# A mean over rows on one core: the first load issued in four parts of rows, and a branch hint for SyncE

## The chip, the cores and the metric

The kernel runs on one core of a Trainium2 chip. The metric is the device time of one execution in microseconds (us); the median of the runs is quoted. The kernel before takes between 1246.0 and 1246.5 us, with one run of 1247.15, so differences of a few tenths can be read, with care.

Some words: an engine *issues* a load; 16 DMA engines then carry it out in *packets*, in most loads here 65,536 B each, all that one partition holds of a block. The *tail* is what is left after the last bytes have landed. A *branch hint* is here an instruction near the start of an engine's program that names the branch at its end.

## The reference

```python
x = np.random.randn(64, 256, 8192).astype(np.float32)   # 536.9 MB
return np.mean(x, axis=2)                               # 16384 means of 8192 numbers
```

## The kernel before

The 16384 rows are taken in 64 blocks of 256 rows: 128 partitions, two rows of 32 KB side by side in each, so 64 KB to a partition and 8.39 MB to a block. Three buffers rotate. All loads are issued by SyncE, which does no sums here; all sums but a few at the end are VectorE's.

```python
x_v = x_f[0 : LB * P * R].rearrange("(p n r) s -> n p r s", p=P, r=R)
...
def load(dst, src, sem):
    ld = untracked(nc.sync.dma_start(out=dst, in_=src))
    ...
    ld.then_inc(sem, 16)

for n in range(LB):
    xt = slots[n % SLOTS]
    ld = load(xt[:], x_v[n], load_sem[n % LOAD_SEMS])
    if n == 0:
        first = ld
    if n < LB - 1:
        loaded(n, dve_sum(res[:, n * R : (n + 1) * R], xt[:]))
    ...   # the last of these blocks is shared with ScalarE
...       # the 64th block comes in pieces that get smaller: 4096, 2048, ... 256 columns
scaled_sum(fin[0][:, 0:1], head[:])
st = store_last(0)
with tc.issue_after(st.ins):
    st = nc.sync.wait_ge(tail_sem[-2], 16)
with tc.issue_after(st.ins):
    st = nc.sync.addr_align(FETCH_BLOCK, offset=0, max_nops=0)
untracked(scaled_sum(fin[1][:, 0:1], fin_in[:, 0 : lastw + k]))._wait_ge(sem, 16)
with tc.issue_after(st.ins):
    last_store = store_last(1)
```

After the build the first load is moved by hand ahead of the barrier that starts the program, so that it is SyncE's first instruction of weight. VectorE gets a branch hint for the branch at its end. `addr_align` in front of the last store is meant to align the place of the store's instruction in SyncE's program.

## Time and profile before

| | before |
|---|---|
| median of 6 runs, us | 1246.15 (1246.05 to 1246.41) |
| span of the profiled run, us | 1244.4 |
| bytes read | 536.87 MB |
| beat of a block in the steady part, us | 19.35 |
| first reduction starts, us | 22.07 |
| first data packet starts, us | 1.02 |

The timeline of VectorE at the start shows the beat. Columns: start, length, engine, line, operation, tiles, shapes, count, and in brackets the idle time before it and what ended it.

```profile
22.07 17.22 DVE L80 TENSOR_REDUCE res<-xt 128x2 f32<-128x16384 f32 x1 [21.07 <-DMA xt<-in_x_dram]
41.40 17.22 DVE L80 TENSOR_REDUCE res<-xt 128x2 f32<-128x16384 f32 x1 [2.11 <-DMA xt<-in_x_dram]
```

VectorE works for 17.22 us and waits for 2.1, every time for a load. The start of its first reduction is therefore a handy clock: whatever the first block loses is seen there, and everything behind it is a fixed beat. The view of SyncE's load line (minimum, median and maximum of an issue in ns) gives what an issue costs:

```profile
L70 SPq DMA_DIRECT2D xt<-in_x_dram x69: 327/328/435, 0.0 to 1202.6; - x69
```

### The profile page before, as it was taken

To read this page: it belongs to the slowest core of one execution; us is meant where nothing else is said; L and a number is where in the kernel's file an instruction comes from. 1 tells how busy PE (TensorE), PEld (TensorE's weight loads), DVE (VectorE), ACT (ScalarE), POOL (GpSimd) and SP (SyncE) were. 2 spreads that over 40 slices of the span, in tenths; PEclk is the share of its full clock that TensorE was granted. 3 is DMA by queue.
4 is the path that set the end of the run, shared out by engine and by line. 5 is a ranking of instruction groups with operands and counts; after the bars stand their busy time and mean duration, and the time that the engine had idled before them with its cause. 6 is when DMAs were issued, how large, how long until landed. Compare 5 with 4: busy or idle time off the path is not lost.

```text
span 1244.4 us, 203 instructions
## 1 busy us (share of the span) xinstructions
DVE 1087.0 (87%) x78; ACT 16.5 (1%) x13; POOL 0.2 (0%) x4
## 2 busy tenths in 40 slices
DVE  2898988989889889898898988989889898898898
ACT  0000000000000000000000000000000000000004
POOL 0000000000000000000000000000000000000000
DMA  9999999999999999999999999999999999999998
GB/s 432 423 426 438 438 438 438 436 430 415 438 438 438 438 438 432 417 432 438 438 438 438 432 417 432 438 438 438 438 436 419 426 438 438 438 438 436 426 419 373
DMA packets 10241, 536.95 MB, mean 431 GB/s; under 512 B 1280, under 2 KB 1536, under 8 KB 1792
## 3 DMA queue, kind: packets, MB, share of 16 engines
q1 hardware_dynamic: 10240, 536.94, 99.8%
q14 instruction: 1, 0.01, 0.0%
HBM read 536.87 MB, written 0.07 MB: 431 GB/s over the span
## 4 chain that ended last, share of the span: by engine, by line
DMA 70%; DVE 29%; SPq 0%; issue 0%; DVEq 0%
DMA xt<-in_x_dram 70%; DVE res L80 29%; DVE fin_in L80 0%; SPq L70 0%; DVE fin_in L86 0%; DVE fin_t L97 0%; DVEq L86 0%
## 5 line engine op out<-in xcount | busy, mean ns | idle before, releaser
L80 DVE TENSOR_REDUCE res<-xt 128x2 f32<-128x16384 f32 (+1 forms) x63 | 1076.3, 17085 | 153.1 <-DMA xt<-in_x_dram 153.1
L83 ACT ACT_TABLE_LOAD x1 | 1.3, 1283 | 1181.0 <-DVE res L80 1181.0
L83 ACT ACTIVATE xt<-xt 128x8192 f32<-128x8192 f32 (+5 forms) x6 | 14.7, 2444 | 43.9 <-DMA xt<-in_x_dram 43.7
L80 DVE TENSOR_REDUCE fin_in<-xt 128x1 f32<-128x256 f32 (+3 forms) x5 | 5.0, 1005 | 0.3 <-DMA xt<-in_x_dram 0.2
L80 DVE TENSOR_REDUCE head<-xt 128x1 f32<-128x4096 f32 x1 | 4.4, 4420 | 0.7 <-DMA xt<-in_x_dram 0.7
L83 ACT ACTIVATION_READ_ACCUMULATOR xt<-xt 128x1 f32 x6 | 1.1, 186 | 0.0
L60 DVE MEMSET fin<- 128x32 f32 x2 | 0.1, 85 | 0.9 <-PEq L238 0.9
L86 DVE TENSOR_SCALAR_CACHE_REDUCE fin_in<-fin_in 128x265 f32<-128x265 f32 x1 | 0.4, 430 | 0.2 <-DVE fin_in L80 0.2
L97 DVE STREAM_TRANSPOSE fin_t<-fin 128x32 f32<-128x32 f32 x2 | 0.4, 212 | 0.1
L138 DVE TENSOR_SCALAR bulk<-res 128x126 f32<-128x126 f32 x1 | 0.2, 228 | 0.1
L86 DVE TENSOR_SCALAR_CACHE_REDUCE head<-head 128x2 f32<-128x2 f32 x1 | 0.2, 154 | 0.1
L238 POOL MEMSET const-bfloat16-1.0<- 128x1 bf16 x1 | 0.1, 102 | 0.0
L238 POOL MEMSET const-uint8-127<- 128x1 uint8 x1 | 0.1, 102 | 0.0
L238 POOL MEMSET const-float32-0.0<- 128x1 f32 x1 | 0.1, 99 | 0.2 <-issue 0.2
L238 POOL MEMSET const-float32-1.0<- 128x1 f32 x1 | 0.1, 99 | 0.0
L86 DVE DVE_READ_ACCUMULATOR fin_in<-fin_in 128x1 f32 x1 | 0.1, 83 | 0.0
L86 DVE DVE_READ_ACCUMULATOR head<-head 128x1 f32 x1 | 0.1, 82 | 0.0
## 6 DMA issues: line engine op xcount, KB each, us to landing
xt<-in_x_dram SPq DMA_DIRECT2D x1, 4096.0 KB, 31.2
xt<-in_x_dram SPq DMA_DIRECT2D x1, 2048.0 KB, 35.7
xt<-in_x_dram SPq DMA_DIRECT2D x1, 1024.0 KB, 37.7
xt<-in_x_dram SPq DMA_DIRECT2D x63, 40.8
xt<-in_x_dram SPq DMA_DIRECT2D x1, 512.0 KB, 38.5
xt<-in_x_dram SPq DMA_DIRECT2D x1, 256.0 KB, 38.7
xt<-in_x_dram SPq DMA_DIRECT2D x1, 128.0 KB, 38.6
fin_in<-in_x_dram SPq DMA_DIRECT2D x1, 128.0 KB, 38.5
```

The source lines that it names most:

```text
L60: nc.vector.memset(fin[r][:], 0.0)
L80: return untracked(nc.vector.tensor_reduce(out=dst, in_=src, axis=X, op=ADD))
L83: return untracked(nc.scalar.activation(out=src, in_=src, func=COPY, accum_out=dst))
L86: return nc.vector.tensor_scalar(out=src, in0=src, scalar1=inv, scalar2=None, op0=mybir.AluOpType.mult, op1=ADD, accum_out=dst,)
L97: nc.vector.transpose(out=fin_t[r][:], in_=fin[r][:])
L138: nc.vector.tensor_scalar_mul(out=bulk[:], in0=res[:], scalar1=inv)
L238: nc = _bacc.Bacc("TRN2", target_bir_lowering=False, num_devices=1)
```

## The change

The intent: have the first data sooner by making the first load small, in parts of evenly spaced rows; and replace the wait and the alignment in front of the last store by a hinted branch for SyncE.

```diff
-FETCH_BLOCK = 128
+FIRST_PARTS = ((0, 8), (4, 8), (2, 4), (1, 2))
...
     def loaded(n, ins):
-        ins._wait_ge(load_sem[n % LOAD_SEMS], 16 * (n // LOAD_SEMS + 1))
+        more = len(FIRST_PARTS) - 1 if n % LOAD_SEMS == 0 else 0
+        ins._wait_ge(load_sem[n % LOAD_SEMS], 16 * (n // LOAD_SEMS + 1 + more))
...
-        ld = load(xt[:], x_v[n], load_sem[n % LOAD_SEMS])
-        if n == 0:
-            first = ld
+        for a, step in FIRST_PARTS if n == 0 else ((0, 1),):
+            ld = load(xt[a:P:step], x_v[n, a:P:step], load_sem[n % LOAD_SEMS])
+            if n == 0 and a == 0:
+                first = ld
...
-    with tc.issue_after(st.ins):
-        st = nc.sync.wait_ge(tail_sem[-2], 16)
-    with tc.issue_after(st.ins):
-        st = nc.sync.addr_align(FETCH_BLOCK, offset=0, max_nops=0)
...
# not the code, in short: before, VectorE's closing branch is made a hinted compare-and-branch;
# after, VectorE's and SyncE's, and the first load goes ahead of SyncE's first instruction
# (before: ahead of its drain in front of the start barrier)
```

So the first load becomes rows 0, 8, 16 ... (16 rows), 4, 12, 20 ... (16), 2, 6, 10 ... (32) and 1, 3, 5 ... (64).

More of the change, by code (lines that the diff above doesn't have):

```diff
@@ L157 @@
     head_bb, body_bb = nc.main_func.blocks[:2]
+    blocks = nc.main_func.blocks
+    end_bb, parent = blocks[2], nc.bb_map[body_bb.name]
+    hinted = {e.engine: e for e in (nc.vector, nc.sync)}
+    with nc.body("skipped", parent=parent, valid_engines=[*hinted]):
+        for eng in hinted.values():
+            eng.nop(nofuse=True)
+            eng.br(end_bb.name)
+    with nc.body("scratch", parent=parent, valid_engines=[*hinted]):
+        overs = [
+            eng.br_eq(eng.zero_reg, 0, end_bb.name, "skipped").ins
+            for eng in hinted.values()
+        ]
+    made = {b.name: b for b in blocks}
+    blocks.remove(made["scratch"])
+    blocks.remove(made["skipped"])
+    blocks.insert(2, made["skipped"])
+    for over in overs:
+        made["scratch"].instructions.remove(over)
+        plain = next(
+            i
+            for i in body_bb.instructions
+            if i.engine == over.engine and isinstance(i, mybir.InstUnconditionalBranch)
+        )
+        assert plain.target == end_bb.name
+        body_bb.instructions.insert(body_bb.instructions.index(plain), over)
+        body_bb.instructions.remove(plain)
+        hint = mybir.InstBranchHint(
+            name=nc.get_next_instruction_name(),
+            engine=over.engine,
+            associate_branch=over.name,
+        )
+        at = next(
+            i
+            for i, ins in enumerate(head_bb.instructions)
+            if ins.engine == over.engine and isinstance(ins, mybir.InstDrain)
+        )
+        head_bb.instructions.insert(at, hint)
     assert first.ins in body_bb.instructions
@@ L162 @@
         for i, ins in enumerate(head_bb.instructions)
-        if ins.engine == first.ins.engine and isinstance(ins, mybir.InstDrain)
+        if ins.engine == first.ins.engine
     )
     head_bb.instructions.insert(at, first.ins)
-    DVE = mybir.EngineType.DVE
-    blocks = nc.main_func.blocks
-    end_bb, parent = blocks[2], nc.bb_map[body_bb.name]
-    with nc.body("skipped", parent=parent, valid_engines=[DVE]):
-        nc.vector.nop(nofuse=True)
-        nc.vector.br(end_bb.name)
-    with nc.body("scratch", parent=parent, valid_engines=[DVE]):
-        over = nc.vector.br_eq(nc.vector.zero_reg, 0, end_bb.name, "skipped").ins
-    made = {b.name: b for b in blocks}
-    made["scratch"].instructions.remove(over)
-    blocks.remove(made["scratch"])
-    blocks.remove(made["skipped"])
-    blocks.insert(2, made["skipped"])
-    plain = next(
-        i
-        for i in body_bb.instructions
-        if i.engine == DVE and isinstance(i, mybir.InstUnconditionalBranch)
-    )
-    assert plain.target == end_bb.name
-    body_bb.instructions.insert(body_bb.instructions.index(plain), over)
-    body_bb.instructions.remove(plain)
-    hint = mybir.InstBranchHint(
-        name=nc.get_next_instruction_name(), engine=DVE, associate_branch=over.name
-    )
-    at = next(
-        i
-        for i, ins in enumerate(head_bb.instructions)
-        if ins.engine == DVE and isinstance(ins, mybir.InstDrain)
-    )
-    head_bb.instructions.insert(at, hint)
     exit_ins = list(end_bb.instructions)
```

## The prediction

The sum came to −0.33 us, so 1245.8 us in a range of 1245.1 to 1251.0. Its three terms all stand; the first, −0.40 us, is an estimate from the start times of the packets. Four rivals follow. The first is a lower rate of the small parts (small form: an engine's first two packets double, 20%; large form: all eight, 4%); its doubled packet was an assumption. The second is a first packet that stays as slow as before (25%), the third a wider gain. The fourth: a stall at SyncE's branch (3%). At the end, the signs of the first two rivals come right after those that would show the point right, in the same order.

> **What bounds the kernel now.** I read the page's busy shares and slices first, then its DMA queues, the chain of waits near the end, the stage table in steps of 0.2 us for the first microseconds, and the timeline of the tail.
>
> ```profile
> DVE 1087.0 (87%) x78; ACT 16.5 (1%) x13; POOL 0.2 (0%) x4
> ...
> DMA  9999999999999999999999999999999999999998
> ...
> q1 hardware_dynamic: 10240, 536.94, 99.8%
> ```
>
> The 16 DMA engines are busy for 99.8% of the span; VectorE has 13% to spare. The chain of the page mixes DMA and VectorE, because a load's issue waits for the reduction that frees its buffer. But that load then queues behind two others, so the reductions cost nothing. The timeline shows it: each reduction of a block takes 17.22 us and then VectorE waits 2.13 us for the next block, a beat of 19.35 us for 8.39 MB, or 433.5 GB/s.
>
> ```profile
> 22.05:41.40 19.35, 17.22 (x1) 0.00 (x0) 0.00 (x0) 1.00 1.00 434
> ...
> 600.00:619.35 19.35, 17.22 (x2) 0.00 (x0) 0.00 (x0) 1.00 1.00 434
> ```
>
> 64 blocks at 19.35 us are 1238.4 us of the 1244.4 us span. Only 6.0 us are left: the start before the engines run, and the tail. The change touches those alone. The start (columns: window, its length, VectorE, ScalarE and GpSimd busy, clock, DMA share and GB/s counted by the packets that start there; 328 GB/s is one packet of 65,536 B in 0.2 us):
>
> ```profile
> 0.80:1.00 0.20, 0.12 (x2) 0.00 (x0) 0.00 (x0) 1.00 0.00 0
> 1.00:1.20 0.20, 0.00 (x1) 0.00 (x0) 0.00 (x0) 1.00 9.96 3277
> 1.20:1.40 0.20, 0.00 (x0) 0.00 (x0) 0.00 (x0) 1.00 2.04 655
> 1.40:1.60 0.20, 0.00 (x0) 0.00 (x0) 0.00 (x0) 1.00 1.92 655
> 1.60:1.80 0.20, 0.00 (x0) 0.00 (x0) 0.00 (x0) 1.00 0.89 328
> 1.80:2.00 0.20, 0.00 (x0) 0.00 (x0) 0.00 (x0) 1.00 0.81 328
> ...
> 4.00:4.20 0.20, 0.00 (x0) 0.00 (x0) 0.00 (x0) 1.00 2.27 983
> 4.20:4.40 0.20, 0.00 (x0) 0.00 (x0) 0.00 (x0) 1.00 6.05 2621
> 4.40:4.60 0.20, 0.00 (x0) 0.00 (x0) 0.00 (x0) 1.00 3.02 1311
> 4.60:4.80 0.20, 0.00 (x0) 0.00 (x0) 0.00 (x0) 1.00 0.76 328
> ```
>
> Nothing moves for 1.02 us. Then 10 engines start at once and six straggle, the last at 1.97. The second packets start between 4.08 and 4.79; the last row is one engine alone. The packet records of the trace give a first packet 2.6 to 3.45 us and every later one 2.414 us. So each engine [...] keeps its lag to the end. The engine that began its second packet at 4.79 sets the end. Taking 2.414 off, it is as if it had begun at 2.37, and what its first packet loses is paid once, in full.
>
> ```profile
> 1240.87 0.79 DVE fin_in L80 x2
> 1241.66 0.03 issue
> 1241.69 0.05 DVEq L86
> 1241.74 0.07 issue
> 1241.80 0.45 DVE fin_in L86 x2
> 1242.25 0.02 issue
> 1242.27 0.21 DVE fin_t L97
> ```
>
> This is the chain at the end: last landings, two small sums, the scaled sum, the transpose. SyncE's last store is issued at 1242.52 for 0.52 us, lands at 1244.06 by the semaphore records, and GpSimd's closing barrier ends the span at 1244.43.
>
> [...] 433.5 GB/s, or 65,536 B in 2.414 us = 27.1 GB/s (10^9) an engine. [...] The trace has one instruction packet (8192 B at 1242.33, just after VectorE's hinted branch), and no stall beside it.
>
> **The change part by part.**
>
> *First load in parts.* It removes one issue of 128 rows and adds four, of 16, 16, 32 and 64 rows; bytes and packets of 64 KB stay (8 for each engine). The first part has one packet an engine. The order of instructions shows it ahead of the start barrier, as the whole load was, and the other three behind it. An issue takes 0.33 to 0.43 us in the trace, whatever the size, and the first packet started 0.63 us after the first issue ended (1.02 − 0.40); the last store also has 0.64. So I leave the first start at 1.02. What can shrink is the straggling and the long first packet. The engine that started last, at 1.97, needed only 2.60 us, 0.18 over the steady 2.41, while early starters needed 0.6 to 1.0 more. [...] If the straggling halves (0.95 to about 0.5) and the least excess of 0.18 to 0.6 holds, the slowest engine's effective start is 1.02 + 0.5 + 0.18 to 0.6 = 1.7 to 2.1 in place of 2.37. I take −0.40 us, all of it on the path.
>
> *Does the second part come in time?* It is issued behind the barrier, at about 0.9 in place of 0.80 for the second block's issue now, so its packets are ready near 0.9 + 0.33 + 0.63 = 1.9. The first packets last beyond 3.5. The third and fourth issues end before 2.2. No gap.
>
> *Three more completions.* At a block's end the packet spacing is 2.420 in place of 2.414 us, so one completion costs an engine 6 ns: +0.02 us.
>
> *SyncE's hint and register move in front of the start barrier.* SyncE arrives there last already (its drain ends at 0.57), so the barrier moves by some 0.1 us. VectorE's first reduction starts at 22.07, so this lies beside the load: 0.
>
> *The closing wait and alignment go.* They stood in front of the last store and were done at 1241.32, before the store's release at 1242.50. Removed, they free nothing. The store may lose what the alignment bought: the unaligned store of the other half took 0.637 us, the aligned last one 0.522. This 0.115 would be on the path; I count half, +0.05.
>
> *SyncE's compare and branch.* The two in the trace took 33 and 78 ns. SyncE's last drain ended at 1243.56, 0.5 us ahead of the landing that the closing barrier waits for: 0.
>
> Sum: −0.40 + 0.02 + 0.05 = −0.33; 1246.09 − 0.33 = 1245.76, say 1245.8.
>
> **The rivals.**
>
> [...] a packet takes 4.83 instead of 2.41 us. This adds 2 × 2.41 = 4.8 us, less the 0.4: about 1250.5. [...] all eight packets double: 19.3 us more, 1265. [...] I give 20% to the small form and 4% to the large one.
>
> [...] Then all 16 engines still finish their first packets between 4.1 and 4.8, and only the tail moves: 1246.1 to 1246.2. For it: the ten engines that start together are slower than the late ones[...]. 25%.
>
> *A wider gain.* If all engines begin like the best do now (4.08), the end moves by 0.71 us, to 1245.4. With a shorter issue for 16 rows, 1245.1. That is the floor that I believe in.
>
> [...]
>
> **Range and chances.** About half the weight is on 1245.4 to 1246.0, a quarter on no change, a quarter above, most of it near 1250.5. The point follows the likeliest case. The low end is the floor; [...] the range is lopsided: 1245.1 to 1251.0. Two per cent is 25 us, more than start and tail hold together (6 us)[...]. Faster by over 2%: 0.4%; slower: 1%; within: 98.6%.
>
> **What would show it.** Right: the window table shows 16 packets starting by about 1.5 us, second packets all before 4.5, first reduction at 21.6 to 21.8 instead of 22.07, the beat still 19.35, and the tail from the last landing unchanged within 0.15. [...] packets of the first block last 4.8 us, the second wave starts near 6, the first reduction at 26 or later. [...] second packets again up to 4.8 and the first reduction at 22.07. Wrong altogether: a beat other than 19.35, or a span that ends with SyncE's drain later than the store's landing.

## The result, and the profile after

| | before | after |
|---|---|---|
| median of 6 runs, us | 1246.15 | 1251.34 (1251.24 to 1251.39) |
| span of the profiled run, us | 1244.4 | 1249.5 |
| first reduction starts, us | 22.07 | 27.13 |
| beat, us | 19.35 | 19.35 |

The changed kernel is 5.2 us slower, a ratio of 1.0041 (interval 1.0028 to 1.0054). The verdict at 2% is "same"; the loss is still far outside the noise.

The DMA queue line of the page and the timeline of VectorE at the start, after:

```profile
q1 hardware_dynamic: 10288, 536.94, 99.8%
```

```profile
27.13 17.22 DVE L82 TENSOR_REDUCE res<-xt 128x2 f32<-128x16384 f32 x1 [25.64 <-DMA xt<-in_x_dram]
46.47 17.22 DVE L82 TENSOR_REDUCE res<-xt 128x2 f32<-128x16384 f32 x1 [2.12 <-DMA xt<-in_x_dram]
```

The engines are "busy" for the same 99.8%: a busy share does not say at what rate. The 48 packets more are small ones (1328 under 512 B in place of 1280), 16 for each of the three loads more. The first reduction is 5.06 us late, and from there the beat is the old one. So nearly all of the loss lies in the first block. The stage table (the columns are those of the prediction; the last is the rate, counted by the packets that start in a window, so the windows are laid from one wave of packets to the next):

```profile
1.20:1.40 0.20, 0.03 (x1) 0.00 (x0) 0.00 (x0) 1.00 0.00 0
1.40:1.60 0.20, 0.09 (x2) 0.00 (x0) 0.00 (x0) 1.00 13.94 2949
1.60:1.80 0.20, 0.00 (x0) 0.00 (x0) 0.00 (x0) 1.00 3.13 655
...
1.40:5.70 4.30, 0.09 (x2) 0.00 (x0) 0.00 (x0) 1.00 1.13 244
5.70:10.60 4.90, 0.00 (x0) 0.00 (x0) 0.00 (x0) 1.00 1.01 214
10.60:13.90 3.30, 0.00 (x0) 0.00 (x0) 0.00 (x0) 1.00 0.87 318
13.90:16.30 2.40, 0.00 (x0) 0.00 (x0) 0.00 (x0) 1.00 1.01 437
```

Each of the first four waves is 16 packets of 64 KB. The first starts at 1.43 us instead of 1.02. The first and the second run at about half the rate (244 and 214 GB/s); the third is a mixture; from the fourth on the rate is full. The packet records say the same for single packets: median 4.97 us, 4.92 us, 2.84 us, then 2.42 us, where before it was 3.16 us and then 2.42. (The 2.414 us of the prediction is the time from one packet's start to the next in the first blocks; the records are 2.418 us long, and an eighth of the beat is 2.419.) The two slow waves are exactly the two parts of 16 rows.

The issue line of SyncE, and the end of the chain of waits:

```profile
L71 SPq DMA_DIRECT2D xt<-in_x_dram x72: 327/328/640, 0.0 to 1207.7; - x72
```

```profile
1246.80 0.07 issue
1246.87 0.45 DVE fin_in L88 x2
1247.32 0.02 issue
1247.34 0.21 DVE fin_t L99
```

The longest issue is now 640 ns; it is the very first one, where it had been 397. At the end the same pieces stand in the same lengths, 5.07 us later. From the start of the last transpose to the end of the span it is 2.20 us (before 2.15), 0.05 us more. The experiments show that the new tail is not what costs it.

### The profile page after: what moved, and what is told of

Same layout as the page of the kernel before. It is cut to its first block, busy times and chain, and to the rows that moved or that the text cites. A ratio compares the mean times of both kernels' runs of the same rounds, so it can differ in the third digit from the quotient of the medians.

```text
span 1249.5 us, 206 instructions
## 1 busy us (share of the span) xinstructions
DVE 1087.0 (87%) x78; ACT 16.5 (1%) x13; POOL 0.2 (0%) x4
## 2 busy tenths in 40 slices
DMA packets 10288, 536.94 MB, mean 430 GB/s; under 512 B 1328, under 2 KB 1584, under 8 KB 1840
## 3 DMA queue, kind: packets, MB, share of 16 engines
q1 hardware_dynamic: 10288, 536.94, 99.8%
## 4 chain that ended last, share of the span: by engine, by line
DMA 70%; DVE 29%; SPq 0%; issue 0%; DVEq 0%
DMA xt<-in_x_dram 70%; DVE res L82 29%; SPq L71 0%; DVE fin_in L82 0%; DVE fin_in L88 0%; DVE fin_t L99 0%; DVEq L88 0%
```

## The experiments

The theory after the result: the rate of a load depends on which partitions it *writes*. Where a text goes on with figures after [...], they are what this theory expects (one exception is named below). Rivals: the addresses that a part *reads*, now eight times as far apart; small parts that are slow in themselves, or cold at the start; and the tail, with its hint and branch. The trace carries no number of the DMA engine; packets are told apart by their times.

### Which half of the change

`e1_tail_only`: the changed kernel with `FIRST_PARTS = ((0, 1),)`, which is one whole load.

> The changed kernel with the first load whole again, so that only the hint for SyncE, its register move and branch, and the missing wait and alignment remain. [...] the parts make the whole loss, so 1246.1 to 1246.3 us here, with the last store's issue at 0.52 to 0.64 us. If the hint or branch costs something of size: over 1247.

Measured: 1246.31 us (1246.13 to 1246.85) beside 1246.26 for the kernel before, ratio 1.0002 (0.9985 to 1.0019). The last store's issue took 0.514 us although it was no longer aligned, and the last transpose stood 2.14 us before the end (before 2.15).

`e2_parts_only`: the kernel before, with the four parts alone.

```diff
+FIRST_PARTS = ((0, 8), (4, 8), (2, 4), (1, 2))
...       # and the count that the sums wait for, as in the change
-        ld = load(xt[:], x_v[n], load_sem[n % LOAD_SEMS])
+        for a, step in FIRST_PARTS if n == 0 else ((0, 1),):
+            ld = load(xt[a:P:step], x_v[n, a:P:step], load_sem[n % LOAD_SEMS])
```

> The kernel before with the four parts alone (old tail, no hint for SyncE). [...] 1251.2 to 1251.4 us, the loss whole, and with the former run additive. The start barrier, without hint and move of SyncE in front, should end some 0.2 us earlier than in the changed kernel and that should cost or gain nothing.

Measured: 1251.35 us beside 1246.26, ratio 1.0041. The parts are the whole loss, and SyncE's hint, move and branch cost nothing that the times show. The old tail took 2.19 us here, with an aligned last store of 0.552, so the 0.05 us above came with the parts and not with the new tail; why is open. One detail was missed: the start barrier released SyncE at 1.20 us here and at 1.21 in the changed kernel, not 0.2 apart; SyncE's drain ended at 1.05 and at 1.06.

### Written rows or read rows

`e4_src_runs`: written rows as in the change, read rows in runs (wrong result).

```diff
-            ld = load(xt[a:P:step], x_v[n, a:P:step], ...)
+            ld = load(xt[a:P:step], x_v[n, (lo := {8: a * 4, 4: 32, 2: 64, 1: 0}[step]) : lo + P // step], ...)
```

> The destination rows of the four parts stay 0, 8, 16 ... as in the changed kernel, but the source rows of each part are taken in one run (0 to 15, 16 to 31, 32 to 63, 64 to 127), so rows come out permuted and the result is wrong on purpose. [...] nothing changes, the first two packets of an engine last about 4.9 us, the first reduction starts near 27.1 us, the time is about 1251.3 us. Reading addresses in HBM (rival): the row pitch within a part falls to an eighth, the first packets go to 2.4 to 3.4 us and the time to about 1246.

Measured: 1251.75 us in one look, beside 1246.02. The second wave in its stage table:

```profile
5.50:10.45 4.95, 0.00 (x0) 0.00 (x0) 0.00 (x0) 1.00 1.00 212
```

The half rate stays although the read rows are next to each other.

`e5_dst_runs`: the mirror, read rows as in the change, written rows in runs (wrong result).

```diff
+            ld = load(xt[(lo := {8: a * 4, 4: 32, 2: 64, 1: 0}[step]) : lo + P // step], x_v[n, a:P:step], ...)
```

> The mirror of the former: source rows strided as in the changed kernel, destination rows in runs (wrong result on purpose). [...] the first two packets of an engine last about 9.7 us; [...] the other six last about 4.8 us. The first block takes 2 x 9.66 + 6 x 4.83 = 48.3 us in place of 19.3, first reduction near 51 us, time about 1275 us. Reading addresses: as the changed kernel, 1251.3 us. Parts with few descriptors are slow in themselves: also 1251.3 us. If the issue is longer (0.64 us) because rows are strided in the buffer, it returns to about 0.4 us here.

Measured: 1275.84 us beside 1246.02. The second wave, rows 16 to 31:

```profile
8.10:17.40 9.30, 0.00 (x0) 0.00 (x0) 0.00 (x0) 1.00 1.00 113
```

The rate is 113 GB/s, about a quarter of the 434 of the steady part. The packet records give 9.26 us in the median to a packet of this wave, and 4.96 to 5.12 us to packets four to eight. The first reduction started at 51.72 us. Together the two runs settle it: with the same rows read, the rate follows the rows written. The reads are worth no more than some 0.4 us here (1251.75 beside 1251.34, the former a single run).

### Which rows are fast

`e6_low64`: two runs of 64 rows, 0 to 63 and 64 to 127. `e7_mid64`: the runs 32 to 95, 0 to 31, 96 to 127. Both results are right.

```diff
-FIRST_PARTS = ((0, 8), (4, 8), (2, 4), (1, 2))
+FIRST_PARTS = ((0, 64), (64, 128))                  # e6_low64
+FIRST_PARTS = ((32, 96), (0, 32), (96, 128))        # e7_mid64
-            ld = load(xt[a:P:step], x_v[n, a:P:step], ...)
+            ld = load(xt[lo:hi], x_v[n, lo:hi], ...)
```

> Two parts of 64 rows in runs: 0 to 63, then 64 to 127 (a right result). [...] all eight packets of an engine last about 4.83 us, so the block takes 19.3 us more: about 1265.4 us, first reduction near 41 us. Few descriptors (rival): 64 rows gave full rate as the fourth part of the changed kernel, so about 1246 us.

> Parts 32 to 95, 0 to 31, 96 to 127 (a right result). [...] 32 to 95 is a run of 64 rows too, [...] its four packets an engine go at 2.42 us; the two runs of 32 rows [...] their four packets take 4.83 us. Block 9.7 us longer: about 1255.8 us, first reduction near 31.7. If it is the run of 64 rows that is slow, whatever its place: the first part is as slow as in the run of rows 0 to 63, about 4.83 us a packet, and the time is about 1265.

Measured: 1267.78 and 1257.13 us, beside 1246.02. The stage table of the run with 0 to 63 first, over most of its first block:

```profile
5.70:41.20 35.50, 0.00 (x0) 0.00 (x0) 0.00 (x0) 1.00 1.00 207
```

and of the run with 32 to 95 first, its packets two to four, then the two runs of 32 rows:

```profile
4.40:11.60 7.20, 0.00 (x0) 0.00 (x0) 0.00 (x0) 1.00 1.01 437
11.60:31.10 19.50, 0.00 (x0) 0.00 (x0) 0.00 (x0) 1.00 1.01 215
```

This is the cleanest pair. Both first parts are a run of 64 rows, 4 MB. Rows 0 to 63 go at half rate (207 GB/s), rows 32 to 95 at the full one (437 GB/s, 2.42 us a packet). Only the place differs. Both times are over what I had computed, by 2.4 and 1.3 us: most packets of the slow runs took 5.12 us, not 4.83. The expectation is thus right in its pattern, and my packet time was about 6% short here.

### Parts of every fourth and every second row

`e3_parts32`: `FIRST_PARTS = ((0, 4), (1, 4), (2, 4), (3, 4))`. `e8_step2`: `FIRST_PARTS = ((0, 2), (1, 2))`.

The last case of the first text is a first packet as slow as before, whatever the number of rows.

> Four parts of 32 rows (0, 4, 8 ...; 1, 5, 9 ...; and so on), a right result. [...] full rate, packets of 2.4 us from the second on, time between 1245.6 and 1246.6 us. If more and smaller parts are slow by themselves: about 1250 or more. If fewer descriptors let the engines start earlier, as I predicted, the second packets start before 4.5 us everywhere and the time is under 1246; [...] they start at 4.1 to 4.8 us plus the later first issue (0.4 us): about 1246.5 us.

> Two parts of 64 rows (even, then odd), [...] a right result; beside the run of rows 0 to 63 it has the same number of rows and descriptors. [...] full rate, 1245.6 to 1246.6 us. Rows in halves slow by themselves: 1265 as with rows 0 to 63. Issue longer because rows are strided in the buffer: about 0.64 us for the first issue, first packet 0.2 to 0.4 us later than before.

Measured: 1246.63 and 1246.61 us beside 1246.26, ratios 1.0004 (0.9987 to 1.0020) and 1.0003 (0.9986 to 1.0019). Stage table and timeline of the four parts of 32 rows:

```profile
6.90:21.40 14.50, 0.00 (x0) 0.00 (x0) 0.00 (x0) 1.00 1.00 434
```

```profile
22.36 17.22 DVE L82 TENSOR_REDUCE res<-xt 128x2 f32<-128x16384 f32 x1 [20.91 <-DMA xt<-in_x_dram]
```

Four parts of every fourth row cost nothing of the 5 us. But they gain nothing either: the first reduction is 0.28 us *later* than before (0.46 with two parts). The first issue took 0.587 us here and 0.584 with two parts, against 0.397 for the whole load. The first packets took 3.09 and 3.13 us in the median (before 3.16). So 32 or 64 rows in place of 128 do not make a first packet shorter.

### The slow parts last

`e9_parts_last`: `FIRST_PARTS = ((1, 2), (2, 4), (0, 8), (4, 8))`, with the odd rows moved to SyncE's start in place of rows 0, 8, 16 ...; a right result.

> The same four parts in the reverse order: 64 odd rows, 32, and the two parts of 16 rows last; a right result. [...] the loss goes along with the two parts of 16 rows, so packets 1 to 6 of an engine go at about 2.42 us, 7 and 8 at about 4.92, and the time stays at 1251.3 to 1251.7 us. If the loss is one of the start (small parts leave the engines without work, or a cold start), the first packets are slow or nothing is, and the time falls to about 1246.6.

Measured: 1251.87 us beside 1246.12, ratio 1.0046; 0.2 us over the range expected. Packets two to six, then seven and eight:

```profile
4.40:16.50 12.10, 0.00 (x0) 0.00 (x0) 0.00 (x0) 1.00 0.99 428
16.50:25.70 9.20, 0.00 (x0) 0.00 (x0) 0.00 (x0) 1.00 1.05 228
```

The loss moved to the end of the block together with the two parts of 16 rows. So it does not belong to the start.

### Where the first packet loses its time

`e10_cols`: the first load in three parts of columns, 128 rows each. `e11_halves`: in two. `e12_halves_old_tail`: the latter in the kernel before.

```diff
+FIRST_PARTS = ((0, 0, 2048), (0, 2048, 8192), (1, 0, 8192))   # e10_cols
+FIRST_PARTS = ((0, 0, 8192), (1, 0, 8192))                    # e11_halves, e12_halves_old_tail
+        for r, lo, hi in FIRST_PARTS if n == 0 else ((slice(0, R), 0, S),):
+            ld = load(xt[:, r, lo:hi], x_v[n, :, r, lo:hi], ...)
```

> The first load in three parts along the columns, 128 rows each (8 KB, 24 KB and 32 KB a row), a right result; it shows in finer steps where the first packet loses its time. [...] no loss of 5 us: 1246.0 to 1246.6 us. If the 0.6 to 1.0 us that a first packet takes over 2.41 us is a delay before the first bytes, the first packets of 8 KB last 0.6 us or more over their 0.30 and the following ones are at 0.30, and the time is as before or up to 0.2 us more. If it grows with the size of the first packet (a rush that slows it all along), it is spread over many packets or shrinks, and the time falls by up to 0.4 us.

> The first load as two parts of 128 rows, one of the two rows of 32 KB that a partition holds in each; a right result. Fixed delay before the first bytes: as the kernel before, 1246.2 to 1246.5 us. Delay that grows with the packet: 1245.8 to 1246.1.

> The kernel before with the first load in two halves of 32 KB a row, 128 rows each, and nothing else: the one candidate that may beat it. In the profile of the halves with the new tail the first reduction came 0.30 us earlier than before, but between the eighth and the tenth block 0.2 us went again in one step and the end was the same. If that step was an accident of that one execution: first reduction near 21.8 us, beat 19.351 all along, 1245.8 to 1246.0 us. If an early start is always given back: 1246.1 to 1246.3.

Measured: 1246.48 us (1245.96 to 1246.90) and 1246.22 us (1246.11 to 1246.34), beside 1246.12; and 1246.27 us beside 1246.16. None is faster, the ratios are 1.0001, 1.0000 and 1.0000, each with an interval of about 0.0015 to either side. With 8 KB packets the records show the loss in the first few of an engine (up to 0.71 us), and most later ones at 0.31. That fits neither a pure delay before the first byte nor a slowing all along: it is a spell, from the first packet at 1.02 us to about 2.6 us, in which some packets of nearly every engine are slow. Its cause is not settled.

The four runs of `e10_cols` fall in two pairs, 1245.96 and 1246.13, 1246.82 and 1246.90. The profile is of one of the slow pair: a 24 KB packet at 4.48 us took 1.64 us where the others take 0.91, and the first reduction came at 22.56. The fast pair has no profile, so this run doesn't show what an undisturbed start in columns is worth.

The halves did start earlier: the first reduction at 21.78 us with the new tail and 21.84 with the old, 0.2 to 0.3 before the 22.07 of the kernel before. Both profiles then lose most of it again in one step, at a place that differs (near 200 and near 130 us). The second, and the same stretch of the kernel before below it:

```profile
118.65 17.22 DVE L82 TENSOR_REDUCE res<-xt 128x2 f32<-128x16384 f32 x1 [2.17 <-DMA xt<-in_x_dram]
138.21 17.22 DVE L82 TENSOR_REDUCE res<-xt 128x2 f32<-128x16384 f32 x1 [2.34 <-DMA xt<-in_x_dram]
```

```profile
118.80 17.22 DVE L80 TENSOR_REDUCE res<-xt 128x2 f32<-128x16384 f32 x1 [2.13 <-DMA xt<-in_x_dram]
138.15 17.22 DVE L80 TENSOR_REDUCE res<-xt 128x2 f32<-128x16384 f32 x1 [2.13 <-DMA xt<-in_x_dram]
```

One beat was 19.56 us in place of 19.35, and the lead of 0.15 us became a lag of 0.06. In these two runs single packets reached 2.62 us, where the kernel before has none over 2.44 after its start. In these two the engines also ran closer together (0.24 to 0.41 us between the first and the last, before 0.7). That alone is not why they are disturbed: in the profile of `e10_cols`, where one engine is more than 1 us apart from the rest, packets near 70 us reached 2.61. All three loads split by columns show such packets; of the loads split by rows, only `e3_parts32` has any over 2.44 after 60 us, two of them, the longer 2.49. Why is open.

No version beats the kernel before.

## Why the prediction was wrong

**What bounds the kernel**: right. The first block's loss came through to the end one to one (first reduction 5.06 us late, last transpose 5.07, span 5.1), and the beat did not move.

**The steps that failed**: the sum −0.40 + 0.02 + 0.05 gave the first two parts no term of their own, so it took their packets to run at the full rate of the steady part. Its point lies 5.6 us under the measured time. Of these, some 4.7 us are packets of the first block that took 4.97, 4.92 and 2.84 us in place of 3.16, 2.42 and 2.42; the other 0.8 us are the start, 0.41 later where 0.40 earlier was forecast.

**The likeliest case, a start that is 0.40 us better**: wrong, the smaller of the two: "If the straggling halves (0.95 to about 0.5) and the least excess of 0.18 to 0.6 holds". That fewer rows would do this was my estimate, and no trace showed it. The first packet takes 3.0 to 3.2 us in the median with 128, 64 and 32 rows alike (`e1_tail_only`, `e7_mid64`, `e8_step2`, `e3_parts32`). So the number of rows is not what it waits for, as far as 32 to 128 rows show it; in the parts of 16 the slow packets (4.97 us) hide it. Its companion, "So I leave the first start at 1.02", fell too: I had taken an issue to last 0.33 to 0.43 us whatever the size. The part of 16 rows took 0.640, and its first packet came 0.79 us after the issue's end and not 0.63. That is 0.41 us lost in place of 0.40 won.

**The rival of a lower rate**: the larger step, left out of the sum; that the rate goes by the rows written is shown (the second wave at 212 GB/s in `e4_src_runs`, at 113 in `e5_dst_runs`), and it had only 20%. The sum of its small form was 4.8 − 0.4. Its terms as measured, medians over the 16 packets of a wave: first packet 4.97 − 3.16 = 1.81, second 4.92 − 2.42 = 2.50, third 2.84 − 2.42 = 0.42, together 4.73, and the later start 0.41; the sum is 5.14 and the first reduction shows 5.06. So its term was right in size. The 0.4 that I took off as a gain should have been added, and this alone put the result beyond the high end of 1251.0.

**Why I gave it too little weight**: I took a claim made for the change, that each DMA engine keeps its rows, as a fact; the traces have no number of the engine and don't show which rows it carries. The full rate of the loads of 128 partitions (434 GB/s) says nothing of a load that writes fewer. The runs show which sets of rows are slow: 16 rows at step 8 (`after`, 214 GB/s), a run of 16 (`e5_dst_runs`, 113), the runs 0 to 31 and 96 to 127 (`e7_mid64`, 215) and the runs 0 to 63 and 64 to 127 (`e6_low64`, 207). And they show which are not: 32 rows at step 4 (`e3_parts32`, 434), 64 at step 2 (`after`, its packets from 16.3 us on, 437), the run 32 to 95 (`e7_mid64`, 437). The trap of the change is that an even spread looks safe: sixteen rows spread over all partitions (244 and 214 GB/s) ran about as slow as runs of 32 rows (215). What makes a set slow was not shown; the records give rates by rows, and all 16 packets of a wave are in flight at once.

**The large form of the rival** (all eight packets double): wrong, the third and fourth part ran at full rate (437 GB/s), but for 0.42 us in the third packet. The second and third rival, **a first packet as slow as before** and **a wider gain**, concern the start: with 32 to 128 rows the first packet stayed slow (3.0 to 3.2 us), as the former said, and the reason is open; the latter did not come.

**Second part in time, three completions, start barrier**: right in effect. The second packets followed the first within 0.02 us. The barrier came 0.5 us later (SyncE's drain ended at 1.06, not 0.57), more than I had said, and nothing waited for it.

**The tail**: +0.05 us estimated, 0.05 us in the profiles of the two kernels, but for another reason, so this was luck. `e1_tail_only`, with the new tail and one whole first load, shows nothing of it; `e2_parts_only`, with the old tail, shows 0.04. The last store's issue was 0.562 us in the changed kernel and 0.514 in `e1_tail_only`, both unaligned, 0.552 in `e2_parts_only` and 0.522 before, both aligned. So the alignment bought nothing that could be seen here: the 0.637 us from which the prediction took its 0.115 belongs to the other half's store, which takes as long (0.638 us) in the changed kernel. SyncE's branch took 70 ns and its last drain ended at 1248.66, 0.55 us ahead of the end of the wait for the store's landing.

**Chances**: within 2% held, for the reason given: start and tail together are 6 us, and 2% is 25.

## What to carry to other kernels

When a load of 128 partitions is split, choose the rows of each part by the partitions that they write, and measure the rate of each part: here the sets of rows went at 113 to 437 GB/s. Evenly spaced is not enough; 16 rows at step 8 halved the rate of two megabytes (214 and 244 GB/s) and cost 5 us, while four parts of 32 rows at step 4 ran at full rate (434 GB/s). The choice of halves matters as well: rows 0 to 63 and 64 to 127 cost 21.8 us over 1246.02, even and odd rows 0.35 us over 1246.26. With DMA engines busy for 99.8%, such a split had nothing to win here unless the start really waited for the size of the first load. That can be measured first, by one run with a smaller first load at step 2 or 4 (`e3_parts32` and `e8_step2` are such runs: 0.4 us slower).

## Measured here and not explained

- The time of an issue by its shape: as first instruction 0.397 us where 128 rows are written (`before`), 0.58 to 0.64 us for 16, 32 or 64 strided rows (`after` 0.640, `e3_parts32` 0.587, `e8_step2` 0.584).
- The slow first packet of an engine: 3.0 to 3.2 us in the median against 2.42.
- A start earlier by 0.2 to 0.3 us was lost again, most of it, within 200 us in both profiles that had one.
